# A fifth pair of k tiles in the seven-product scheme of six units of a transformer block kernel

## The chip, the core and the metric

The kernel runs on one core of a Trainium2 chip. The metric is the device time of one launch in microseconds; lower is better. The kernel before took 1368.11 us, the median of three runs (1367.73, 1368.11 and 1368.4).

## The reference, cut to what matters

One block of a hybrid encoder over 256 tokens and 2048 channels, all in float32: a normed input goes through one wide projection, a gated recurrence and a banded attention run side by side, their outputs are merged by gates and projected, and an MLP with a squared ReLU follows. The change lies in the MLP, which is about half of the time:

```python
u = rms_norm(h, norm_mlp_w[l])
h = h + jnp.square(jax.nn.relu(u @ w_up[l])) @ w_down[l]     # (256,2048)@(2048,8192), (256,8192)@(8192,2048)
return rms_norm(h, norm_final_w)
```

## The kernel before

**Three matmuls for one product.** Each float32 factor is split into a rounded part (`wh`, or `hi` on the token side) and the rest (`wl`, `lo`), and `mm3` (L139 to L142) adds hi·wh, hi·wl and lo·wh: L140, L141 and L142, always in that order. One matmul is 128x128 by 128x512.

**Splitting the weights.** A raw block of weights, 128x1024 float32 or 512 KB (two k tiles by 512 columns), comes by one DMA that SyncE (SP) issues (`piece`, L216). ScalarE (ACT) casts it to `wh` (L91), VectorE (DVE) subtracts to get `wl` (L92); `parts` (L221) does this, in buffers that `buf` (L202) hands out. `wh` and `wl` have four buffers each; after the gates' units begin, every fifth block gets a buffer in a further pool, `fifths`, so that there are five. The cast of a block can't start before TensorE (PE) has read the last of the block whose buffer it takes.

**A unit** (`class Unit`, L782, and `run`, L895) makes a 256x1024 output over 16 k tiles: 2 by 2 output banks c11, c12, c21, c22. The first 8 k tiles go through a seven-product scheme of Strassen's kind: with the k tiles as two halves of four, each product is four k tiles times 512 columns, and the unit needs 7 of them, 7 x 4 x 3 = 84 matmuls, where 8 would be the plain way. They are named by bank and weight block, in this order: 11A, 22A, then 12C and 11D (either first), 21A, 21B, 21D. The weight blocks A, B, C, D are two raw tiles each, numbered 0 and 2. DVE adds A += B and A += C in place (`sums`, L851, L854); GpSimd (POOL) sends B += C and D += A as adding DMAs (`sent`, L856). On the token side the combinations are the tiles S5, S4, S2 and S7 made by `combos` (L743). k tiles 8 to 15 go the plain way, two at a time for both token halves: 8 items (`ITEMS`, L780) of 12 matmuls, shown as r1_8, r0_12 and so on (column half, first k tile). That is 84 + 96 = 180 matmuls for a unit.

**Order.** It is written out in `run`, and Tile's scheduler moves what `high_priority` and `issue_after` let it. The last two items of a unit (k tiles 12, 13 and 14, 15 of the second column half) are kept in the list `late` and run inside the next unit, behind its products 11A and 22A; they cover the ACT copies of c11 into c21 and c22 into c12 (`begun`, L831, through L812). When all outputs of a unit are there, ACT evicts them: a ReLU and a square for the up projection (L1208, L1209), a copy `y` for the down projection (L1219), which POOL adds to memory.

**The units of the MLP** follow one another as up00, up02, dn00, dn02, up10, up12, dn10, dn12, up20, up22, dn20, dn22, up30, up32, dn30, dn32: four quarters of the 8192 hidden channels, each with two units up and two down. In the second up and the first down unit of a quarter PE also turns the hidden activations (`turns`, L1189; L110), and ACT and DVE split them. `finals` (L1263) loads the last norm's weights in dn30.

Of the kernel before, what the change touches and what calls it, by code (L numbers as in the profile page):

```python
# [50 lines left out]
def tile_hybrid_block(  # L51
# [691 lines left out]
    def combos(lhs, what, home, made, blocks=None):  # L743

        a = {}

        def block(m, j):
            if blocks:
                a[m, j] = blocks[m, j]
                return  # L750
            a[m, j] = fours(token(f"a{m}{j}_{what}"))
            x = lhs[j][:, :, :, m * P:(m + 1) * P].bitcast(F32)
            nc.vector.tensor_tensor(a[m, j], x[:, :, 0, :], x[:, :, 1, :], op=ALU.add)

# [26 lines left out]

    class Unit:  # L782


        def __init__(self, lhs, S, w, n0, what, done, kt0=0, apart=NC, steps=lambda: (), start=5, fresh=None, held=False, tail=False):
# [4 lines left out]
            self.raw, self.dma, self.c, self.items, self.steps = {}, {}, {}, list(ITEMS), []  # L790

        def load(self, name):
# [3 lines left out]
                              for g in (0, 2)]  # L796

# [97 lines left out]
    def run(u, then=None):  # L895
# [18 lines left out]
        if not late and not u.spread:  # L914
# [24 lines left out]
        u.plain(1, (8, 9))  # L939
# [10 lines left out]
        u.plain(1, (10, 11))  # L950
# [6 lines left out]
        if then:  # L957
            then.load("B")
            then.load("C")
        u.step(next(at))  # L960
        u.plain(0, (8, 9))
# [4 lines left out]
        u.plain(0, (10, 11))  # L966
# [5 lines left out]
        if then:  # L972
            then.load("D")
        if u.tail:
# [22 lines left out]
        late.append(lambda: u.plain(1, LATE[0]))  # L997
# [4 lines left out]
    for f in combos(xT, "x", tk, Sx):  # L1002
# [82 lines left out]

    homes["fifth"] = ctx.enter_context(tc.tile_pool(name="fifths", bufs=1, reuse_waits="tile"))
# [52 lines left out]
    def h_blocks(n0):  # L1139

        def one(n, m):
# [7 lines left out]
            with tc.high_priority(offset=2000):  # L1149
                nc.vector.tensor_tensor(tmp, tp, bc(wmlp[:, 4 * n:4 * n + 4], 2, P), op=ALU.mult)  # L1150
                split(hi[:, :, m * P:(m + 1) * P], lo[:, :, m * P:(m + 1) * P], tmp)
# [33 lines left out]
    for qd in range(NQ):  # L1185
# [3 lines left out]
        def turns(c0, uT=uT, rs=rs, Su=Su, blocks=blocks, qd=qd):  # L1189

            def one(c, m):
# [7 lines left out]
                split(hi[:, :, m * P:(m + 1) * P], lo[:, :, m * P:(m + 1) * P], tp)  # L1199

            return [(c, lambda c=c, m=m: one(c, m)) for c in (c0, c0 + 1) for m in range(NM)] + [
                (c0 + 1, f, 7) for f in ([] if c0 else combos(uT, f"u{qd}", tk, Su, blocks))]

        for c in range(0, 4, 2):
            def done(m, n, acc, c=c, rs=rs, qd=qd):
                t = token(f"r{qd}{c}{n}{m}")
                with tc.high_priority(offset=2000):
# [5 lines left out]
                              steps=(lambda turns=turns: turns(0)) if c else (lambda: ()) if qd else (lambda: h_blocks(2)), start=3 if c else 0, held=not qd and not c))  # L1213
# [49 lines left out]
        def finals():  # L1263
# [3 lines left out]
            nc.scalar.activation(fin["w"], fin["w"], AF.Copy, scale=D ** 0.5)  # L1267
# [4 lines left out]

        for n0 in (0, 2):
            units.append(Unit(lambda uT=uT: uT, lambda Su=Su: Su, w_down, n0 * NC, f"dn{qd}{n0}",
                              lambda m, n, acc, *c, n0=n0, out_of=out_of: out_of(m, n0 + n, acc, *c), kt0=qd * KD,
                              steps=(lambda: ()) if n0 else (lambda turns=turns, last=last: turns(2) + [(3, finals)] * last),
                              start=0, tail=last and n0 == 2))

    for u, then in zip(units, units[1:] + [None]):
# [45 lines left out]
```

## Time and profile before

| | us |
|---|---|
| median of three runs | 1368.11 |
| the profiled execution | 1367.7 |
| its span, first to last instruction | 1366.0 |
| PE busy | 1356.6 (99%) |
| DVE busy | 1122.2 (82%) |
| ACT busy | 948.5 (69%) |
| one unit without transposes (up10) | 40.80 |

The profiled execution is 1.7 us longer than its span and 0.4 us below the median. A matmul is listed with 0.39 us, but it overlaps its neighbours: the next one starts 0.23 us later, and it is this step that counts. For DVE and ACT the same holds in a smaller way: in a row of back-to-back operations the steps are a little shorter than the durations.

### The profile page before, as it was taken

The page shows a single profiled execution, that of the slowest core. Times are in us where ns is not written, and L with a number is a line of the kernel's source. Part 1 is how long each engine was busy: PE and PEld are TensorE (multiplying, and loading weights), DVE is VectorE, ACT ScalarE, POOL GpSimd, SP SyncE. Part 2 cuts the span into 40 slices and gives each one's busy share as a digit, 9 for nine tenths or more (in the row PEclk, how much of TensorE's full clock was granted, in tenths as well). Part 3 has the DMA queues.
Part 4 walks back from the last instruction along what each step waited for, and adds up shares of the span by engine and source line. Part 5 has one row for each costly group of instructions (what it writes and reads, how often), then busy time and mean ns, then how long its engine had stood idle before and what let it go on. Part 6 is the DMA issues. An engine that isn't in the chain of part 4 may idle for free.

```text
span 1366.0 us, 19039 instructions
## 1 busy us (share of the span) xinstructions
PE 1356.6 (99%) x6787; PEld 1123.0 (82%) x6787; DVE 1122.2 (82%) x1302; ACT 948.5 (69%) x1247; POOL 150.1 (11%) x231
## 2 busy tenths in 40 slices
PE   9999999999999999999999999999999999999997
PEld 8888888878778888888888888888888888888886
DVE  7888977887788775798998987789787888878885
ACT  6877765776777664456678766687666876668864
POOL 4000000111111000010121111100111002110210
PEclk9999999999999999999999999999999999999999
DMA  9655557788886996569899889998899888998892
GB/s 333 240 186 156 181 177 264 216 221 244 260 225 169 293 296 210 182 154 324 284 265 269 235 260 295 283 256 244 250 278 298 250 253 237 286 296 258 269 281 98
DMA packets 128895, 333.75 MB, mean 244 GB/s; under 512 B 11152, under 2 KB 12176, under 8 KB 128416
## 3 DMA queue, kind: packets, MB, share of 16 engines
q1 hardware_dynamic: 108080, 265.85, 56.2%
q0 software_dynamic: 20144, 66.14, 24.7%
q8 instruction: 53, 0.87, 0.2%
q10 hardware_dynamic: 576, 0.55, 0.1%
q14 instruction: 42, 0.34, 0.1%
HBM read 271.67 MB, written 10.49 MB: 207 GB/s over the span
## 4 chain that ended last, share of the span: by engine, by line
PE 99%; DMA 1%; ACT 0%; POOLq 0%; issue 0%; POOL 0%
PE acc_hq L182 2%; PE acc_hf L182 2%; PE tp_u L110 1%; PE acc_hg L142 1%; PE acc_hi L142 1%; PE acc_hg L140 1%; PE acc_bb L140 1%; PE acc_hi L141 1%; PE acc_hf L187 1%; PE acc_ba L142 1%; PE acc_hg L141 1%; PE acc_bb L142 1%; PE acc_ba L140 1%; PE acc_ba L141 1%; PE acc_hi L140 1%; PE acc_bb L141 1%
## 5 line engine op out<-in xcount | busy, mean ns | idle before, releaser
L182 PE MATMUL acc_hf<-act_x,wh_hf 128*128 128x512 f32 x128 | 40.9, 401 | 0.6 <-ACT wh_hf L91 0.6
L182 PE MATMUL acc_hq<-act_x,wh_hq 128*128 128x512 f32 x128 | 40.8, 399 | 0.2 <-ACT wh_hq L91 0.2
L91 ACT CAST wh_bb<-raw_bb 128x1024 fp32r<-128x1024 f32 x16 | 16.9, 1054 | 23.3 <-PE acc_ba L142 17.7
L92 DVE TENSOR_TENSOR wl_bb<-raw_bb,wh_bb 128x1024 fp32r<-128x1024 f32 x16 | 19.6, 1223 | 14.8 <-ACT wh_bb L91 14.8
L91 ACT CAST wh_ba<-raw_ba 128x1024 fp32r<-128x1024 f32 x16 | 16.9, 1053 | 19.9 <-PE acc_bb L142 13.8
L92 DVE TENSOR_TENSOR wl_ba<-raw_ba,wh_ba 128x1024 fp32r<-128x1024 f32 x16 | 19.6, 1223 | 10.8 <-ACT wh_ba L91 10.8
L187 PEld LDWEIGHTS acc_hf<-act_x,wl_hf 128*128 128x128 f32 x128 | 23.4, 189 | 5.7 <-DVE wl_hf L92 0.5
L187 PEld LDWEIGHTS acc_hq<-act_x,wl_hq 128*128 128x128 f32 x128 | 23.4, 188 | 5.2
L1220 POOL DMA_DIRECT2D hd<-y x24 | 26.2, 1171 | 1.8 <-ACT y L1219 1.3
L92 DVE TENSOR_TENSOR act_u<-tp_u,act_u 128x512 fp32r<-128x512 f32 x32 | 21.9, 684 | 4.7 <-ACT act_u L91 4.2
L140 PE MATMUL acc_bb<-wh_bb,act_yb 128*128 128x512 f32 x64 | 25.2, 393 | 0.0
L140 PE MATMUL acc_hg<-wh_hg,act_x 128*128 128x512 f32 x64 | 25.1, 392 | 0.0
L140 PE MATMUL acc_hi<-wh_hi,act_x 128*128 128x512 f32 x64 | 25.0, 391 | 0.0
L142 PE MATMUL acc_hg<-wh_hg,act_x 128*128 128x512 f32 x64 | 24.9, 390 | 0.0
L142 PE MATMUL acc_ba<-wh_ba,act_ya 128*128 128x512 f32 x64 | 24.9, 389 | 0.0
L142 PE MATMUL acc_hi<-wh_hi,act_x 128*128 128x512 f32 x64 | 24.9, 389 | 0.0
L141 PE MATMUL acc_hi<-wl_hi,act_x 128*128 128x512 f32 x64 | 24.9, 389 | 0.0
L141 PE MATMUL acc_hg<-wl_hg,act_x 128*128 128x512 f32 x64 | 24.9, 389 | 0.0
L140 PE MATMUL acc_ba<-wh_ba,act_ya 128*128 128x512 f32 x64 | 24.9, 389 | 0.0
L141 PE MATMUL acc_ba<-wl_ba,act_ya 128*128 128x512 f32 x64 | 24.9, 389 | 0.0
L141 PE MATMUL acc_bb<-wl_bb,act_yb 128*128 128x512 f32 x64 | 24.9, 389 | 0.0
L142 PE MATMUL acc_bb<-wh_bb,act_yb 128*128 128x512 f32 x64 | 24.9, 389 | 0.0
(1996 smaller groups left out, 5220.2 us busy)
## 6 DMA issues: line engine op xcount, KB each, us to landing
raw_hi<-in_w_in_n_dram SPq DMA_DIRECT2D x16, 512.0 KB, 4.2
raw_hg<-in_w_in_n_dram SPq DMA_DIRECT2D x16, 512.0 KB, 3.6
raw_ba<-in_w_branch_a_dram SPq DMA_DIRECT2D x16, 512.0 KB, 4.5
raw_bb<-in_w_branch_b_dram SPq DMA_DIRECT2D x16, 512.0 KB, 4.5
raw_hf<-in_w_in_t_dram SPq DMA_DIRECT2D x12, 512.0 KB, 4.1
raw_hq<-in_w_in_t_dram SPq DMA_DIRECT2D x12, 512.0 KB, 5.3
hd<-y POOLq DMA_DIRECT2D x24, 256.0 KB, 7.5
raw_aq<-in_w_in_t_dram SPq DMA_DIRECT2D x8, 512.0 KB, 4.5
```

What stands on the lines that cost most here:

```text
L91: casts[:] = [(copy or nc.scalar.copy)(hi, src)]
L92: low[:] = [nc.vector.tensor_tensor(lo, src, hi.bitcast(F32), op=ALU.subtract)]
L110: nc.tensor.transpose(tp[:, j, :], src[:, j * P:(j + 1) * P], ident)
L140: nc.tensor.matmul(acc, hi, wh, start=first, stop=False, skip_group_check=True)
L141: nc.tensor.matmul(acc, hi, wl, start=False, stop=False, skip_group_check=True)
L142: newest[:] = [nc.tensor.matmul(acc, lo, wh, start=False, stop=last, skip_group_check=True)]
L182: newest[:] = [nc.tensor.matmul(acc[cb], wh[:, cb * P:(cb + 1) * P], r.rearrange("p u t -> p (u t)"), start=kt == 0, stop=last)]
L187: newest[:] = [nc.tensor.matmul(acc[cb][:, 0:T], wl[:, cb * P:(cb + 1) * P], r[:, 0, :], start=False, stop=False)]
L1220: nc.gpsimd.dma_start(hd[n][m], t, accum_op=ALU.add)
```

## The change

Six units (up10, up20, up30, dn02, dn12 and dn22) take a fifth pair of k tiles into the seven products: k tiles 8 and 9. Each product then has five k tiles, 15 matmuls, and only 6 plain items stay (`ITEMS5`): 7 x 15 + 6 x 12 = 177 matmuls.

- The weights of k tiles 8 and 9 come as two raw blocks of 512 KB: X (k tile 8: A5 and B5) and Y (k tile 9: D5 and C5), each 512 columns of a block. They lie in the `fifths` pool, in the place of the fifth `wh` and the fifth `wl` buffer (`load5`). So from unit dn00 to unit up30, eleven units, the split buffers are four and not five (`homes["extra"]`).
- Each product has a third, half-wide split of 128x512 (`half`), which takes a whole buffer.
- The sums of the fifth blocks are DVE additions of 128x512 (`add5`): A5 += B5, A5 += C5, D5 += A5, B5 += C5.
- On the token side `fifths` makes the fifth combinations, one tile S9, once for h (in dn02) and once a quarter for the hidden activations (in dn00, dn10, dn20). Its place is that of S7, which moves into a part of the split activations that no product reads (token half 1 of the first four k tiles). That part is therefore not split any more for h and the hidden activations, and for x S7 is made after the product that still reads it.
- A five-pair unit leaves one late item for the next unit and not two; the next unit then runs 11D ahead of 12C. The addition A += C is placed behind the first of these two products.
- `finals` no longer scales the last norm's weights; a step behind it does (`rooted`).

```diff
-    homes = {}
+    homes = {"extra": False}
...
-        if "fifth" in homes:
-            taken[tag] += 1
-        last = taken[tag] > 0 and taken[tag] % 5 == 0
+        taken[tag] += homes["extra"]
+        last = homes["extra"] and taken[tag] % 5 == 0
...
+    def half(raw, what):
+
+        made = [buf(t, what)[:, 0:NC] for t in ("wh", "wl")]
+        with tc.high_priority(offset=2000):
+            lows.append(split(*[t.rearrange("p (c n) -> p c n", n=T) for t in made], raw))
+        return made
...
-            t = home.tile([P, 4, 2, P], F32R, name=f"S{i}_{what}", tag=f"S{i}", bufs=1)
+            if i == 7:
+                t = lhs[0][:, :, :, P:2 * P]
+            else:
+                t = home.tile([P, 4, 2, P], F32R, name=f"S{i}_{what}", tag=f"S{i}", bufs=1)
...
+    def fifths(lhs, what, home, made):
+
+        a = token(f"a9_{what}").rearrange("p (j t) -> p j t", t=T)
+        x = lhs[2][:, 0:2].bitcast(F32)
+        nc.vector.tensor_tensor(a, x[:, :, 0, :], x[:, :, 1, :], op=ALU.add)
+        c = fours(token(f"c9_{what}"))
...
+        t = home.tile([P, 4, 2, P], F32R, name=f"S9_{what}", tag="S7", bufs=1)
+        split(t[:, :, 0, :], t[:, :, 1, :], c)
+        for k, i in enumerate((5, 7, 2, 4)):
+            made[i].append([t[:, k, u, :] for u in range(2)])
...
+    ITEMS5 = [(1, (10, 11)), (1, (12, 13)), (0, (10, 11)), (0, (12, 13)), (0, (14, 15)), (1, (14, 15))]
+    SUMS5 = {("22", "A"): ("A", "B"), ("21", "A"): ("A", "C"), ("21", "B"): ("B", "C")}
...
+        def load5(self, name):
+            if not self.five:
+                return
+            raw = homes["fifth"].tile([P, 2 * NC], F32, name=f"raw5{name}_{self.what}", tag=("wh", "wl")[name == "Y"], bufs=1)
+            ncols = self.w.shape[-1]
+            k, kpr = self.kt0 + 8 + (name == "Y"), 4 * NC // ncols
+            nc.sync.dma_start(raw.rearrange("p (c n) -> p c n", n=ncols),
+                              self.w[self.n0 // ncols:(self.n0 + 2 * NC) // ncols, k // kpr, :, k % kpr, :].rearrange("c p n -> p c n"))
+            for i, block in enumerate({"X": "AB", "Y": "DC"}[name]):
+                self.raw[f"{block}5"] = raw[:, i * NC:(i + 1) * NC].rearrange("p (c n) -> p c n", n=T)
+
+        def add5(self, dst, src):
+            dst, src = [self.raw[f"{name}5"] for name in (dst, src)]
+            with tc.issue_after(lows[-1].ins), tc.high_priority(offset=2000):
+                nc.vector.tensor_tensor(dst, dst, src, op=ALU.add)
...
+                if not g and self.five and (i, name) in SUMS5:
+                    self.add5(*SUMS5[i, name])
                 for a in range(2):
                     mm3(self.c[i], *left(g + a), wh[:, a], wl[:, a], first and not g + a, False)
+            if self.five:
+                mm3(self.c[i], *left(4), *half(self.raw[f"{name}5"], f"{self.what}p{i}{name}5"), False, False)
+                if (i, name) == ("21", "A"):
+                    self.add5("D", "A")
...
-        if not late and not u.spread:
+        if len(late) < 2 and not u.spread:
             seconds.reverse()
...
         seconds[0]()
+        behind_first = lows[-1]
         u.step(next(at))
         seconds[1]()
         with ExitStack() as es:
-            if u.spread:
-                es.enter_context(tc.issue_after(lows[-1].ins))
+            if u.spread or u.five:
+                es.enter_context(tc.issue_after((behind_first if u.five else lows[-1]).ins))
             u.sums("A", "C")
...
             then.load("B")
             then.load("C")
+            then.load5("X")
...
         if then:
             then.load("D")
+            then.load5("Y")
...
-        late.append(lambda: u.plain(1, LATE[0]))
+        if not u.five:
+            late.append(lambda: u.plain(1, LATE[0]))
         late.append(rest)
...
-                split(hi[:, :, m * P:(m + 1) * P], lo[:, :, m * P:(m + 1) * P], tp)
+                if c or not m:
+                    split(hi[:, :, m * P:(m + 1) * P], lo[:, :, m * P:(m + 1) * P], tp)
...
+        def rooted():
+            with tc.issue_after(casts[0].ins):
+                nc.scalar.activation(fin["w"], fin["w"], AF.Copy, scale=D ** 0.5)
...
-    for u, then in zip(units, units[1:] + [None]):
+    lent = [i for i, u in enumerate(units) if u.five]
+    for i, (u, then) in enumerate(zip(units, units[1:] + [None])):
+        homes["extra"] = not lent[0] - 1 <= i <= lent[-1]
         run(u, then)
```

How the instructions stand, at two places of unit up10. First DVE, from the splits of the third product on; `wl_up10p12C0` is the split of the weight tile C0 for product 12C, `wl_up10r1_8` that of a plain item, `raw_up10A2<-raw_up10A2,raw_up10C2` an addition A += C. Before:

```order
L92 TENSOR_TENSOR wl_up10p22A2_8042<-raw_up10A2_7831,wh_up10p22A2_8041 128x1024
L92 TENSOR_TENSOR wl_dn02r1_14_8054<-rawp_dn02r1_14_7899,wh_dn02r1_14_8053 128x1024
L854 TENSOR_TENSOR raw_up10A2_7831<-raw_up10A2_7831,raw_up10C2_7880 128x1024
L92 TENSOR_TENSOR wl_up10p12C0_8078<-raw_up10C0_7878,wh_up10p12C0_8077 128x1024
L92 TENSOR_TENSOR wl_up10p12C2_8088<-raw_up10C2_7880,wh_up10p12C2_8087 128x1024
L92 TENSOR_TENSOR wl_up10p11D0_8098<-rawd_up10D0_7937,wh_up10p11D0_8097 128x1024
L92 TENSOR_TENSOR wl_up10p11D2_8108<-rawd_up10D2_7939,wh_up10p11D2_8107 128x1024
L92 TENSOR_TENSOR wl_up10r1_8_8122<-rawp_up10r1_8_7973,wh_up10r1_8_8121 128x1024
L92 TENSOR_TENSOR wl_up10p21A0_8140<-raw_up10A0_7829,wh_up10p21A0_8139 128x1024
```

And in the changed kernel, from the split of 22A's fifth tile (A5, in the X block) to that of 21A0:

```order
L92 TENSOR_TENSOR wl_up10p22A5_8119<-raw5X_up10_7942,wh_up10p22A5_8118 128x512
L92 TENSOR_TENSOR wl_up10p11D0_8130<-rawd_up10D0_7988,wh_up10p11D0_8129 128x1024
L92 TENSOR_TENSOR wl_up10p11D2_8140<-rawd_up10D2_7990,wh_up10p11D2_8139 128x1024
L92 TENSOR_TENSOR wl_up10p11D5_8150<-raw5Y_up10_7992,wh_up10p11D5_8149 128x512
L905 TENSOR_TENSOR raw_up10A0_7883<-raw_up10A0_7883,raw_up10C0_7938 128x1024
L92 TENSOR_TENSOR wl_up10p12C0_8157<-raw_up10C0_7938,wh_up10p12C0_8156 128x1024
L92 TENSOR_TENSOR wl_up10p12C2_8167<-raw_up10C2_7940,wh_up10p12C2_8166 128x1024
L92 TENSOR_TENSOR wl_up10p12C5_8177<-raw5Y_up10_7992,wh_up10p12C5_8176 128x512
L905 TENSOR_TENSOR raw_up10A2_7885<-raw_up10A2_7885,raw_up10C2_7940 128x1024
L92 TENSOR_TENSOR wl_up10r1_10_8188<-rawp_up10r1_10_8026,wh_up10r1_10_8187 128x1024
L92 TENSOR_TENSOR wl_up10p21A0_8206<-raw_up10A0_7883,wh_up10p21A0_8205 128x1024
```

The late item r1_14 has left this place, 11D stands ahead of 12C, two half-wide splits have come in, and both additions A += C now stand in front of the first plain item's split, one of them right in front of it.

Second PE, at the same first plain item of up10. Before, from the last matmuls of 11D:

```order
L140 MATMUL acc_up10c11_7985<-wh_up10p11D2_8107,act_h1_6333 128x512
L141 MATMUL acc_up10c11_7985<-wl_up10p11D2_8108,act_h1_6333 128x512
L142 MATMUL acc_up10c11_7985<-wh_up10p11D2_8107,act_h1_6333 128x512
L140 MATMUL acc_up10c12_8051<-wh_up10r1_8_8121,act_h2_6618 128x512
L141 MATMUL acc_up10c12_8051<-wl_up10r1_8_8122,act_h2_6618 128x512
L142 MATMUL acc_up10c12_8051<-wh_up10r1_8_8121,act_h2_6618 128x512
```

And in the changed kernel, from the fifth tile of 12C (with S9 on the token side):

```order
L140 MATMUL acc_up10c12_8125<-wh_up10p12C5_8176,S9_h_7849 128x512
L141 MATMUL acc_up10c12_8125<-wl_up10p12C5_8177,S9_h_7849 128x512
L142 MATMUL acc_up10c12_8125<-wh_up10p12C5_8176,S9_h_7849 128x512
L140 MATMUL acc_up10c12_8125<-wh_up10r1_10_8187,act_h2_6613 128x512
L140 MATMUL acc_up10c22_8096<-wh_up10r1_10_8187,act_h2_6613 128x512
L140 MATMUL acc_up10c21_8066<-wh_up10p21A0_8205,S2_h_6444 128x512
L141 MATMUL acc_up10c12_8125<-wl_up10r1_10_8188,act_h2_6613 128x512
L142 MATMUL acc_up10c12_8125<-wh_up10r1_10_8187,act_h2_6613 128x512
```

Two matmuls that need only `wh` have been moved ahead of the first that needs r1_10's `wl`: it is now the fourth of the item's row and not the second.

## Rows read from the trace of the kernel before

**Rows 1.** The page: busy time of PE, and its granted clock in 40 slices.
```profile
PE 1356.6 (99%) x6787; PEld 1123.0 (82%) x6787; DVE 1122.2 (82%) x1302; ACT 948.5 (69%) x1247; POOL 150.1 (11%) x231
PEclk9999999999999999999999999999999999999999
```

**Rows 2.** The page: the chain that ended last, by engine.
```profile
PE 99%; DMA 1%; ACT 0%; POOLq 0%; issue 0%; POOL 0%
```

**Rows 3.** Waits of PE, whole span: us in total, times, longest.
```profile
PE ps_warm L81 <- DVE warm L79: 1.1, 1, 1.1
PE acc_hf L182 <- ACT wh_hf L91: 0.6, 1, 0.6
PE acc_hq L182 <- ACT wh_hq L91: 0.2, 1, 0.2
```

**Rows 4.** Windows of up10, up12, dn10, ga0: busy us (instructions), PEclk, DMA share, GB/s.
```profile
851.38:892.18 40.80, 40.80 (x181) 33.78 (x180) 31.21 (x28) 27.39 (x31) 6.82 (x8) 1.00 0.98 279
892.18:935.01 42.83, 42.83 (x197) 35.31 (x196) 38.95 (x41) 34.44 (x46) 3.40 (x4) 1.00 0.85 249
935.01:977.73 42.72, 42.72 (x197) 35.35 (x196) 35.49 (x34) 31.32 (x39) 3.85 (x5) 1.00 0.88 249
336.11:383.92 47.81, 47.81 (x241) 38.48 (x240) 38.41 (x44) 35.91 (x56) 5.81 (x11) 1.00 0.84 235
```

**Rows 5.** Timeline of PE in up10: start us, us, engine, line, operation.
```profile
862.26 0.39 PE L140 MATMUL acc_up10c<-wh_up10p12C,S_h 128*128 128x512 f32 x1
862.49 0.39 PE L141 MATMUL acc_up10c<-wl_up10p12C,S_h 128*128 128x512 f32 x1
...
864.98 0.39 PE L140 MATMUL acc_up10c<-wh_up10p11D,act_h 128*128 128x512 f32 x1
...
867.93 0.39 PE L141 MATMUL acc_up10c<-wl_up10r,act_h 128*128 128x512 f32 x1
```

**Rows 6.** Timeline of ACT in up10; in brackets idle us before, and what ended it.
```profile
862.46 0.59 ACT L1219 COPY y<-acc_dn02c 128x512 f32<-128x512 f32 x1 [0.64 <-PE acc_dn02c L142]
862.95 1.05 ACT L91 CAST wh_up10r<-rawp_up10r 128x1024 fp32r<-128x1024 f32 x1
...
865.18 1.06 ACT L91 CAST wh_up10p21A<-raw_up10A 128x1024 fp32r<-128x1024 f32 x1 [0.24 <-PE acc_up10c L142]
```

**Rows 7.** Timeline of DVE in up10.
```profile
854.29 1.22 DVE L92 TENSOR_TENSOR wl_dn02r<-rawp_dn02r,wh_dn02r 128x1024 fp32r<-128x1024 f32 x1
855.43 1.22 DVE L854 TENSOR_TENSOR raw_up10A<-raw_up10A,raw_up10C 128x1024 f32<-128x1024 f32 x1
856.57 1.22 DVE L92 TENSOR_TENSOR wl_up10p12C<-raw_up10C,wh_up10p12C 128x1024 fp32r<-128x1024 f32 x1
...
864.03 1.23 DVE L92 TENSOR_TENSOR wl_up10r<-rawp_up10r,wh_up10r 128x1024 fp32r<-128x1024 f32 x1 [1.44 <-ACT wh_up10r L91]
```

**Rows 8.** Timeline of DVE in up12: operations of 512 columns.
```profile
917.38 0.68 DVE L92 TENSOR_TENSOR act_u<-tp_u,act_u 128x512 fp32r<-128x512 f32 x1
917.98 0.69 DVE L842 TENSOR_TENSOR acc_up12c<-acc_up12c,u_up 128x512 f32<-128x512 f32 x1
918.57 1.21 DVE L92 TENSOR_TENSOR wl_up12r<-rawp_up12r,wh_up12r 128x1024 fp32r<-128x1024 f32 x1
```

**Rows 9.** Timeline of unit ga0, which has four buffers: a split, and its reader.
```profile
337.97 1.23 DVE L92 TENSOR_TENSOR wl_ga0p22A<-raw_ga0A,wh_ga0p22A 128x1024 fp32r<-128x1024 f32 x1 [0.56 <-ACT wh_ga0p22A L91]
...
340.42 0.39 PE L141 MATMUL acc_ga0c<-wl_ga0p22A,S_x 128*128 128x512 f32 x1
```

**Rows 10.** Timeline of PE in up12: the transposes.
```profile
908.51 1.03 PE L110 MATMUL tp_u<-ident,r 128*128 128x128 f32 x8
909.30 0.48 PE L140 MATMUL acc_up12c<-wh_up12r,act_h 128*128 128x512 f32 x1
909.61 0.40 PE L141 MATMUL acc_up12c<-wl_up12r,act_h 128*128 128x512 f32 x1
```

**Rows 11.** Loads: one DMA group of the page's kind, and raw_up10A's time to landing.
```profile
rawp_up10r<-in_w_up_dram SPq DMA_DIRECT2D x8, 512.0 KB, 6.5
...
DMA to landing us min/median/max: 5.6/6.9/11.3
```

**Rows 12.** Timeline of ACT in dn30: the last norm's weights.
```profile
1292.74 1.91 ACT L1267 ACTIVATE wf<-wf 128x2048 f32<-128x2048 f32 x1
```

More of the change, by code (lines that the diff above doesn't have):

```diff
@@ L780, in tile_hybrid_block, with __init__ @@
     ITEMS = [(1, (8, 9)), (1, (10, 11)), (0, (8, 9)), (0, (10, 11)), (0, (12, 13)), (0, (14, 15))] + [(1, ks) for ks in LATE]
+    ITEMS5 = [(1, (10, 11)), (1, (12, 13)), (0, (10, 11)), (0, (12, 13)), (0, (14, 15)), (1, (14, 15))]
+    SUMS5 = {("22", "A"): ("A", "B"), ("21", "A"): ("A", "C"), ("21", "B"): ("B", "C")}
     class Unit:
-        def __init__(self, lhs, S, w, n0, what, done, kt0=0, apart=NC, steps=lambda: (), start=5, fresh=None, held=False, tail=False):
+        def __init__(self, lhs, S, w, n0, what, done, kt0=0, apart=NC, steps=lambda: (), start=5, fresh=None, held=False, tail=False, five=False):
             self.lhs, self.S, self.w, self.n0, self.what, self.done = lhs, S, w, n0, what, done
@@ L789, in __init__ @@
             self.spread, self.fresh = fresh is not None, fresh or ()
-            self.raw, self.dma, self.c, self.items, self.steps = {}, {}, {}, list(ITEMS), []
+            self.raw, self.dma, self.c, self.items, self.steps = {}, {}, {}, list(ITEMS5 if five else ITEMS), []
+            self.five = five
         def load(self, name):
@@ L938, in run @@
         u.step(next(at))
-        u.plain(1, (8, 9))
+        u.plain(1, (10, 11) if u.five else (8, 9))
         item(u)
@@ L949, in run @@
         u.step(next(at))
-        u.plain(1, (10, 11))
+        u.plain(1, (12, 13) if u.five else (10, 11))
         u.less("12", u1)
@@ L959, in run @@
             then.load("C")
+            then.load5("X")
         u.step(next(at))
-        u.plain(0, (8, 9))
+        u.plain(0, (10, 11) if u.five else (8, 9))
         u.less("22", u2)
@@ L965, in run @@
         u.step(next(at))
-        u.plain(0, (10, 11))
+        if not u.five:
+            u.plain(0, (10, 11))
         u.residual("11")
@@ L995, in rest @@
             u.end(1)
-        late.append(lambda: u.plain(1, LATE[0]))
+        if not u.five:
+            late.append(lambda: u.plain(1, LATE[0]))
         late.append(rest)
     Sx = {}
-    for f in combos(xT, "x", tk, Sx):
+    x_sums = combos(xT, "x", tk, Sx)
+    for f in x_sums[:3]:
         f()
@@ L1054, in tile_hybrid_block @@
         scaled("k0", rstd, m, acc_k[m])
+    x_sums[3]()
     yb += [new_act(f"yb{g}") for g in range(2)]
@@ L1150, in one @@
                 nc.vector.tensor_tensor(tmp, tp, bc(wmlp[:, 4 * n:4 * n + 4], 2, P), op=ALU.mult)
-                split(hi[:, :, m * P:(m + 1) * P], lo[:, :, m * P:(m + 1) * P], tmp)
+                if n or not m:
+                    split(hi[:, :, m * P:(m + 1) * P], lo[:, :, m * P:(m + 1) * P], tmp)
             nc.scalar.activation(tp.rearrange("p k t -> p (k t)"), t, AF.Square, accum_out=ssq2[:, m, n:n + 1])
@@ L1198, in one @@
                     nc.scalar.copy(blocks[m, c], tp)
-                split(hi[:, :, m * P:(m + 1) * P], lo[:, :, m * P:(m + 1) * P], tp)
+                if c or not m:
+                    split(hi[:, :, m * P:(m + 1) * P], lo[:, :, m * P:(m + 1) * P], tp)
             return [(c, lambda c=c, m=m: one(c, m)) for c in (c0, c0 + 1) for m in range(NM)] + [
-                (c0 + 1, f, 7) for f in ([] if c0 else combos(uT, f"u{qd}", tk, Su, blocks))]
+                (c0 + 1, f, 7) for f in ([] if c0 else combos(uT, f"u{qd}", tk, Su, blocks))] + [
+                (99, lambda: fifths(uT, f"u{qd}", tk, Su), 7)] * (c0 > 0 and qd < NQ - 1)
         for c in range(0, 4, 2):
@@ L1212, in tile_hybrid_block @@
             units.append(Unit(lambda: hT, lambda: Sh, w_up, qd * (FF // NQ) + c * NC, f"up{qd}{c}", done,
-                              steps=(lambda turns=turns: turns(0)) if c else (lambda: ()) if qd else (lambda: h_blocks(2)), start=3 if c else 0, held=not qd and not c))
+                              steps=(lambda turns=turns: turns(0)) if c else (lambda: ()) if qd else (lambda: h_blocks(2)), start=3 if c else 0, held=not qd and not c, five=qd > 0 and not c))
         def out_of(m, n, acc, c=slice(0, NC), last=last, qd=qd):
@@ L1275, in tile_hybrid_block @@
                               lambda m, n, acc, *c, n0=n0, out_of=out_of: out_of(m, n0 + n, acc, *c), kt0=qd * KD,
-                              steps=(lambda: ()) if n0 else (lambda turns=turns, last=last: turns(2) + [(3, finals)] * last),
-                              start=0, tail=last and n0 == 2))
-    for u, then in zip(units, units[1:] + [None]):
+                              steps=(lambda qd=qd: [(99, lambda: fifths(hT, "h", sp, Sh))] * (not qd)) if n0 else (lambda turns=turns, last=last: turns(2) + [(3, finals), (99, rooted, 9)] * last),
+                              start=3 if n0 else 0, tail=last and n0 == 2, five=n0 == 2 and not last))
+    lent = [i for i, u in enumerate(units) if u.five]
+    for i, (u, then) in enumerate(zip(units, units[1:] + [None])):
+        homes["extra"] = not lent[0] - 1 <= i <= lent[-1]
         run(u, then)
```

9 lines of the change are left out of this document (7 added, 2 removed).

## The prediction

> **What bounds the kernel now.** I began with the page: PE is busy for 1356.6 of 1366.0 us, and its granted clock is at the upper level, 2.4 GHz, in all 40 slices [rows 1]. The chain that ended last is 99% PE [rows 2]. PE's waits, asked for next, are three, 1.9 us in all, none in the MLP [rows 3]. So the time of the MLP is its matmuls by the step from one to the next. The windows give the step; their columns are the length, the busy time of PE, PEld, DVE, ACT and POOL, and the clock, DMA share and GB/s. Unit up10 takes 40.80 us for 180 matmuls: 0.2267 us each [rows 4]. Where PE never waits, a product left out is worth its matmuls, as long as nothing new is late. So I read in timelines how far ahead of PE the splits are.
>
> **How near the splits are.** In up10 the split of the first plain item starts at 864.03, takes 1.23 and ends at 865.26 [rows 7]; PE's first matmul that reads it is at 867.93 [rows 5]. The lead is 2.67 us. Its path: PE leaves the buffer at 862.26 (the next piece's first matmul) [rows 5]; an eviction copy starts at 862.46, 0.20 later, and holds ACT until the cast starts at 862.95; the split starts 1.08 after that [rows 6, 7]. So release to split is 1.28 us without a copy in the way and 1.77 with one; 1.28 agrees with the other cast in the rows, which starts 0.20 after its matmul (864.98, 865.18) [rows 5, 6]. Operations in a row on DVE step by 1.14 us at 1024 columns (854.29, 855.43, 856.57) and by 0.60 at 512 (917.38, 917.98, 918.57) [rows 7, 8]; listed durations are 1.22 and 0.68.
>
> **The change, part by part.**
>
> *Matmuls.* Six units go from 180 to 177: 18 x 0.2267 = -4.08 us. This is the whole gain; a unit should take 40.12.
>
> *DVE in these units.* 22 splits of 1024 become 20, seven of 512 and four additions of 512 come in: -2 x 1.22 + 11 x 0.68 = +5.0 us. With up10's 31.21 [rows 4] that is about 36 of 40.1. ACT gets seven casts of 512 for two of 1024, at most 7 x 0.59 - 2 x 1.05 = +2.0 on 27.39 [rows 4, 6], with 0.59 the duration of a copy. Neither is full on the mean; the question is one tight place.
>
> *The tight place of the up units (up10, up20, up30).* Count from the first matmul of 11A. PE's row, in matmuls: 11A 15, late item r1_14 12, 22A 15, 11D 15, 12C 15, then the item r1_10. With four buffers 11D0 takes that of r1_14, which PE leaves after 27 matmuls, at 6.12 us. With a copy in the way the split of 11D0 starts at 6.12 + 1.77 = 7.89. By the order shown, DVE then has six operations of 1024 (11D0, 11D2, A0 += C0, 12C0, 12C2, A2 += C2) and two of 512 (11D5, 12C5) before r1_10: 7.89 + 6 x 1.14 + 2 x 0.60 = 15.93, and r1_10's split ends at 17.15. PE wants it as the fourth matmul of the item, after 75: 17.00. So it is 0.15 late. On the way 12C0 ends at 7.89 + 3 x 1.14 + 0.60 + 1.22 = 13.13 against 58 matmuls, 13.15: no room either. By the listed durations instead of the steps the row lasts 8.68 and r1_10 ends at 17.79, 0.79 late; were no copy in the way, 0.34 early. So 0 to 0.8 a unit; I take 0.25, nearer to the steps, since back to back is what the rows show. Three units: +0.75. In the kernel before the cover here was the second late item, 12 matmuls or 2.72 us; it is gone.
>
> *The down units (dn02, dn12, dn22)* still get two late items, and 12C goes first. The same sum with 12 more matmuls ahead leaves 11D0, here behind 12C and both additions, some 0.5 early. 0 to 0.3, taken 0.03 each: +0.1.
>
> *Five plain units with four buffers (dn00, up12, dn10, up22, dn20).* Pessimistically, a buffer less costs the lead of one plain item, 12 matmuls: 2.67 - 2.72 = -0.05. But ga0, on four buffers already, is the nearest row: a split there ends at 337.97 + 1.23 = 339.20, its reader is at 340.42, a lead of 1.22 [rows 9], and PE waits nowhere in it [rows 3]. I take 0; 0 to 0.3 each.
>
> *Transposes.* In up12, up22, up32 and up02 fewer items or another order puts the groups as 8 transposes, 8 matmuls, 8 and 4 instead of 8, 10, 4, 1, 4, 1. A group's change costs a little: eight transposes start at 908.51, the next matmul is at 909.30 and the one behind it 0.31 later, not 0.23 [rows 10]. up12 is 42.83 long against up10's 40.80, 2.03 us for 16 transposes [rows 4]; two groups of 0.79 would be 1.58 and a third change 0.1 to 0.2. I take -0.2 in up02 and up32, which have five buffers: -0.4; all four within -1.0 and +0.3.
>
> *Token side.* The fifth combinations are an addition and a split of 512, a cast, and four narrow additions, 2 to 2.5 us of DVE, in dn00, dn10, dn20 and dn02; one split of 0.68 is dropped for h and each quarter. dn10 has 42.72 - 35.49 = 7.2 us of DVE free [rows 4], and nothing reads S9 before the next five-pair unit. 0, bounds 0 and 0.3 each. S7 of x, moved behind another product: 0 for the same reason.
>
> *The norm's weights.* Their scaling, 1.91 us of ACT in dn30 [rows 12], now stands ahead of an activation copy that PE's transposes and combinations hang on. Up to its length less what leads there are: 0 to 0.3, taken 0.1.
>
> *Loads.* Bytes stay. X and Y are issued on SP's queue behind C and D. X's place is free when 21B's half-wide split is done, and X is wanted at least 66 matmuls, 15.0 us, later; blocks of this size land in 6.5 us, at worst 11.3 [rows 11]. Hidden; SP's later loads stand one or two issues further back, with the same lead.
>
> *Sum.* -4.08 + 0.75 + 0.1 - 0.4 + 0.1 = -3.5 us, of which I keep -3.4, for the token side. From the profiled execution's 1367.7 that gives 1364.3; it lies 0.4 below the median, so 1364.7 on the scale of 1368.11.
>
> **The rivals.**
>
> *A: the gain is eaten.* All tight places at their upper ends: three up units x 0.8, three down x 0.3, five plain units x 0.1, the norm 0.3, no gain at the transposes: -4.08 + 2.4 + 0.9 + 0.5 + 0.3 = 0.0; with some of it, 1367.5. For it: 12C0 and r1_10 have no lead by my count. Against it: it needs listed durations where rows show shorter steps.
>
> *B: four buffers are too few (slower).* In a product with a half-wide split the three buffers behind the released one hold 6 + 6 + 3 matmuls, 3.40 us. A new split needs 1.77 + 1.22 = 2.99 from the release [rows 5 to 7]. The margin is 0.41 us; a second copy on ACT (0.49) or one DVE operation ahead (0.60) ends it, and PE then stalls again and again. At 0.3 us in three places in eleven units: +9.9 - 4.1 gives about 1374. It decides from some 14 such stalls on. The whole stretch has the lent buffers, not only the six units. Against it: ga0's wait-free run [rows 3, 9], though it has no half-wide splits, and plain units hold 18 matmuls, 4.08 us, behind a release. The Trainium skill, "Perfetto Trace Analysis", Optimization Strategy, speaks for this rival: the same gap repeating on the engine that should be saturated can mean that there is too little memory for the next tile. No run here shows such gaps yet.
>
> *C: X comes too late (slower).* X is fetched in runs of 1 KiB in the up units where the blocks before had 2 KiB, and the DMA share in up10 is already 0.98 [rows 4]. If a block took twice the worst landing, 22.6 us, PE would stand for 7.6 in each up unit: 1364.7 + 22.8 = 1387; it decides from 15.0 us to landing on. At twice the median, 13.0, nothing is seen. Against it: X is one block in 16, and its lead is over twice the median. The same page's section DMA Optimizations says that transfers under 2 KB carry a significant overhead each; by it X would be slower to land, but it gives no time that could be set against 15.0.
>
> *The change doing nothing* is out: the three matmuls a unit are gone from PE's row.
>
> **How the numbers follow.** Forecast 0.62, A 0.26, B 0.09, C 0.03. What can be told from no change is 0.2%, 2.7 us: faster is below 1365.4, slower above 1370.8. The forecast's own range is 1363.2 (no stall, -0.8 at the transposes) to 1366.0; its upper part, about 0.04, is within 0.2%, and about as much of A and B's lighter sides lies to either side. Faster 0.61, same 0.28, slower 0.11. The range goes on through A to 1368.6 and leaves out B, C and 0.05 below or between.
>
> **What would show it.** Right: from 11A to the next 11A the six units take 40.1 to 40.9 us; PE's new waits are for DVE, on 12C0 or r1_10 in up10, up20 and up30, 0.1 to 0.8 each, and hardly any elsewhere; DVE's busy time in up10 is 35 to 36; up12 and dn10 stay within 0.3 of before. Wrong: waits of PE for a cast in many units (B), ACT waiting for the X or Y block's DMA (C), a granted clock below 1.00 behind a stall, or six units at 40.1 with no wait at all, which would mean that DVE's row is shorter than I counted.

## The result: slower by 0.23%

The changed kernel takes 1371.76 us, the median of 16 runs, against 1368.22 us of the kernel before, 16 runs beside them: a ratio of 1.0023, 95% interval 1.0017 to 1.0030. That is 3.5 us slower where 3.4 us faster were forecast, and 3.2 us above the forecast's range.

The page of the profiled execution still shows PE busy all the time [rows 1], but the chain that ended last is no longer PE alone [rows 2]:

```profile
PE 1356.5 (99%) x6769; PEld 1120.3 (82%) x6769; DVE 1149.2 (84%) x1375; ACT 958.9 (70%) x1276; POOL 150.0 (11%) x231
...
PE 94%; DMA 2%; DVE 1%; ACT 1%; issue 1%; POOL 0%; POOLq 0%; DVEq 0%; ACTq 0%
```

18 matmuls are gone (6769 for 6787), and PE's busy time is the same to 0.1 us: a PE that steps slowly is busy too. The waits of PE name two places that were not there before [rows 3], both in up30 (us in total, times, longest):

```profile
PE acc_up30c L140 <- ACT wh_up30r L91: 1.5, 1, 1.5
PE acc_hf L182 <- ACT wh_hf L91: 1.3, 1, 1.3
PE ps_warm L81 <- DVE warm L79: 1.1, 1, 1.1
PE acc_up30c L141 <- DVE wl_up30r L92: 0.9, 1, 0.9
```

The windows from 11A to the next unit's 11A say how much (up10, up12, dn12, up30; columns as in [rows 4]). A unit's stretch takes in the late items of the unit before: dn12 has two, up10 and up30 one, so up10 and up30 hold 177 matmuls, 40.13 us at 0.2267 each, and dn12 189, 42.85 us. up12 takes in one and leaves two: 168 matmuls, and its 16 transposes.

```profile
854.84:895.28 40.44, 40.44 (x179) 33.07 (x178) 35.79 (x38) 29.87 (x36) 6.92 (x9) 1.00 1.04 294
895.28:935.41 40.13, 40.13 (x186) 33.09 (x184) 37.07 (x39) 33.34 (x45) 3.44 (x5) 1.00 0.90 271
978.13:1020.98 42.85, 42.85 (x191) 35.49 (x190) 36.99 (x39) 30.03 (x36) 6.57 (x9) 1.00 0.93 251
1187.11:1231.99 44.88, 42.40 (x178) 34.02 (x177) 37.60 (x39) 30.08 (x36) 7.55 (x10) 0.96 0.95 268
```

By these counts dn12 has no stall at all, up10 (and up20) 0.3 us, and up30 4.75 us. From dn02's 11A to dn30's the units take 460.06 us against 458.69 before. With 18 matmuls less that stretch should be 4.08 shorter; it is 1.37 longer, so 5.45 us were lost, 4.75 of them in up30. Outside it the profiled execution has 1.4 us more ahead of dn02, 0.1 in dn30 and 0.9 from dn32's start to the end.

What happened in up30 stands in ACT's timeline:

```profile
1216.93 0.62 ACT L91 CAST wh_up30p21D<-raw5Y_up 128x512 fp32r<-128x512 f32 x1
1221.74 2.94 ACT L91 CAST wh_up30r<-rawp_up30r 128x1024 fp32r<-128x1024 f32 x3 [4.19 <-DMA rawp_up30r<-in_w_up_dram]
1224.59 1.99 ACT L91 CAST wh_up32p11A<-raw_up32A 128x1024 fp32r<-128x1024 f32 x2
```

ACT stands for 4.19 us until a load lands, and then makes three casts in a row: the last two items were there, and could not pass. The program's order says which cast stood in front. ACT's row in the changed kernel:

```
L91 CAST wh_up30p21D5_11254<-raw5Y_up30_10914 128x512
L91 CAST wh_up30r1_14_11332<-rawp_up30r1_14_11125 128x1024
L91 CAST wh_up30r0_12_11265<-rawp_up30r0_12_11016 128x1024
L91 CAST wh_up30r0_14_11281<-rawp_up30r0_14_11049 128x1024
```

The first of the three plain items, r1_14, is the late item: it is the unit's last load on SP's queue, and PE needs it last of the three, inside up32. Its cast got the fifth `wh` buffer, which is given back for up32. That is the place of the X block, free as soon as 21B's half-wide split has read X; so, unlike the other two, this cast had no matmul to wait for, and it was put ahead of them. PE then ran dry (timeline of PE):

```profile
1221.88 0.39 PE L142 MATMUL acc_up30c<-wh_up30p21D,act_h 128*128 128x512 f32 x1
1223.79 0.50 PE L140 MATMUL acc_up30c<-wh_up30r,act_h 128*128 128x512 f32 x1 [1.53 <-ACT wh_up30r L91]
1225.24 0.79 PE L141 MATMUL acc_up30c<-wl_up30r,act_h 128*128 128x512 f32 x1 [0.95 <-DVE wl_up30r L92]
1225.83 0.63 PE L142 MATMUL acc_up30c<-wh_up30r,act_h 128*128 128x512 f32 x1
1226.26 0.63 PE L140 MATMUL acc_up30c<-wh_up30r,act_h 128*128 128x512 f32 x1
```

and came back at the lower clock (windows of 1 us; 0.50 is the level of 1.2 GHz):

```profile
1226.00:1227.00 1.00, 1.00 (x4) 0.81 (x3) 1.00 (x2) 0.58 (x1) 0.00 (x0) 0.50 0.88 324
...
1228.00:1229.00 1.00, 1.00 (x5) 0.84 (x4) 1.00 (x2) 0.00 (x0) 0.00 (x0) 0.89 0.96 205
```

The three starts after 1221.88 come 1.91, 1.45 and 0.59 us apart instead of 0.23, 3.3 us beyond the usual; then steps of 0.43 cost another 1.2 us until the clock is back. Sum 4.5, the difference between up30 and up10.

### The profile page after: what moved, and what is told of

Read it like the earlier page. It is cut to its first block, busy times and chain, and to the rows that moved or that the text cites. A ratio compares the mean times of both kernels' runs of the same rounds, so it can differ in the third digit from the quotient of the medians.

```text
span 1369.8 us, 19126 instructions
## 1 busy us (share of the span) xinstructions
PE 1356.5 (99%) x6769; PEld 1120.3 (82%) x6769; DVE 1149.2 (84%) x1375; ACT 958.9 (70%) x1276; POOL 150.0 (11%) x231
## 4 chain that ended last, share of the span: by engine, by line
PE 94%; DMA 2%; DVE 1%; ACT 1%; issue 1%; POOL 0%; POOLq 0%; DVEq 0%; ACTq 0%
PE acc_hq L182 2%; PE acc_hf L182 2%; PE tp_u L110 1%; PE acc_hf L187 1%; PE acc_hg L140 1%; PE acc_hi L140 1%; PE acc_bb L140 1%; PE acc_hi L142 1%; PE acc_hg L142 1%; PE acc_ba L142 1%; PE acc_bb L142 1%; PE acc_ba L140 1%; PE acc_hg L141 1%; PE acc_ba L141 1%; PE acc_bb L141 1%; PE acc_ga2c L140 1%
## 5 line engine op out<-in xcount | busy, mean ns | idle before, releaser
L182 PE MATMUL acc_hq<-act_x,wh_hq 128*128 128x512 f32 x128 | 40.9, 399 | 0.2 <-ACT wh_hq L91 0.2
L187 PE MATMUL acc_hf<-act_x,wl_hf 128*128 128x256 f32 x128 | 24.7, 279 | 0.0
```

Of the source, the lines that this page charges most:

```text
L182: newest[:] = [nc.tensor.matmul(acc[cb], wh[:, cb * P:(cb + 1) * P], r.rearrange("p u t -> p (u t)"), start=kt == 0, stop=last)]
L187: newest[:] = [nc.tensor.matmul(acc[cb][:, 0:T], wl[:, cb * P:(cb + 1) * P], r[:, 0, :], start=False, stop=False)]
```

## The experiments

Theory: a cast out of turn in up30 holds ACT, and that is the whole swing. Rivals: the loads themselves are pushed back by X and Y; four split buffers are too few. The times are medians; the kernel before had 1368.6 us beside the first four, 1368.6 beside the next four and 1369.9 beside the last.

### e1_lent_longer and e2_cast_in_turn: the late item back in its place, two ways

```diff
-        homes["extra"] = not lent[0] - 1 <= i <= lent[-1]
+        homes["extra"] = not lent[0] - 1 <= i <= lent[-1] + 1      # e1
```
```diff
+        held = casts[0].ins                                        # e2
         def rest():
-            u.plain(1, LATE[1])
+            with ExitStack() as es:
+                if u.what == "up30":
+                    es.enter_context(tc.issue_after(held))
+                u.plain(1, LATE[1])
```

> The changed kernel, but the split buffers stay four for one unit more, through up32, so that the late item of up30 gets an ordinary buffer. Theory: the loss sits in up30, where this late item got the fifth buffer, free early; its cast was put ahead of those of r0_12 and r0_14 and ACT, which works in order, stood 4.2 us for its load. Then up30 takes 40.4 us instead of 44.9, no PE wait there, and the kernel some 1367.3 (kernel before 1368.2, changed 1371.8). Rival: the DMA is full (share 0.9 and more) and X and Y push the plain items' loads back; then ACT waits in up30 for another load just as long and the time stays at 1371 to 1372. Second rival, four buffers are too few: a unit more of them makes it worse, 1372 or more.

> The changed kernel; the cast of up30's late item r1_14 may only be issued behind that of r0_14, buffers as in the changed kernel. ACT's row differs in this place and one copy behind it, DVE's in the matching split, nothing in the loads. Theory: up30 40.4 us, no PE wait in it, clock 1.00 throughout, the kernel 1367.3 and its runs closer together than the changed kernel's. Rival (loads pushed back by X and Y): still 1371 or more, since the loads are the same.

e1 took 1367.10 us (ratio to before 0.9989, 0.9981 to 0.9998), e2 1367.18 (0.9994, 0.9985 to 1.0002). In e2 not one load changed its place. On ACT and DVE this cast and its split did, with a few operations of up32 behind them, and on PE one matmul of up32. up30 is as long as up10:

```profile
1187.00:1227.44 40.44, 40.44 (x179) 33.07 (x177) 35.46 (x38) 29.95 (x37) 5.88 (x7) 1.00 1.02 295
```

ACT there takes the items in the order of their loads, held only for its split buffers until the last (timeline of ACT in e2):

```profile
1218.57 1.05 ACT L91 CAST wh_up30r<-rawp_up30r 128x1024 fp32r<-128x1024 f32 x1 [1.35 <-PE acc_up30c L142]
1219.93 1.06 ACT L91 CAST wh_up30r<-rawp_up30r 128x1024 fp32r<-128x1024 f32 x1 [0.30 <-PE acc_up30c L142]
1221.62 1.05 ACT L91 CAST wh_up30r<-rawp_up30r 128x1024 fp32r<-128x1024 f32 x1 [0.63 <-DMA rawp_up30r<-in_w_up_dram]
```

The cast of the late item, the last of these, starts when its load lands, 34.9 us after up30's first matmul; in the changed kernel that was 34.6. So the load did not come sooner; it no longer stood in front. 4.0 (e2) to 4.7 us (e1) of the changed kernel's 1371.8 by the ratios, 4.6 by the medians, hang on the place of one cast. What is left is small: e1 is 0.02 to 0.19% faster than the kernel before, and e2 can't be told from it. That the runs would lie closer together did not come true: e2's go from 1365.4 to 1370.8.

### e3_before_four and e5_before_four_turn: four split buffers alone

```diff
-        if "fifth" in homes:
-            taken[tag] += 1
-        last = taken[tag] > 0 and taken[tag] % 5 == 0
+        taken[tag] += homes["extra"]
+        last = homes["extra"] and taken[tag] % 5 == 0
...
+        homes["extra"] = not 4 <= i <= 14          # units dn00 to up30 (e3, of the kernel before)
```

> The kernel before, without any fifth pair, but with four split buffers from dn00 to up30 as in the changed kernel. PE's row is the same. Theory: four buffers cost nothing to 0.1 us a unit, 1368.2 to 1369.3; in up30 the cast of the late r1_12 moves one place ahead of r0_14's, which may cost ACT about 1 us of waiting and PE nothing. Rival (four buffers too few): PE waits for DVE or ACT in most of the eleven units, 1370 or more.

1376.02 us (ratio 1.0057, 1.0042 to 1.0071): the theory was wrong here. Four buffers in the old layout cost up10 0.9, up12 0.4, up20 0.5, up22 0.5 and up30 3.45 us in the profiled execution (1373.68, the shortest of the six), and the six down units 0 to 0.14 each. In up30 both causes meet, for here too the first late item's cast had moved ahead of r0_14's:

```profile
ACT wh_up30r L91 <- DMA rawp_up30r<-in_w_up_dram: 9.6, 3, 4.0
PE acc_up30c L140 <- ACT wh_up30r L91: 1.4, 1, 1.4
PE acc_up30c L141 <- DVE wl_up30r L92: 0.9, 1, 0.9
```

e5 holds that cast behind r0_14's, as e2 does:

> As e3_before_four (kernel before, four split buffers from dn00 to up30, 1376.0), but in up30 the cast of the late r1_12 comes behind r0_14's, in the order of their loads. Theory of casts out of turn: the 3.45 us that up30 took beyond 40.8 in e3 fall to the 0.5 to 0.9 that up10 and up20 took, so some 2.5 us go and the kernel is at 1373 to 1374. Rival: up30's excess comes from late loads as in up10 and up20 and only grew there; then it stays near 3 and the kernel at 1375 to 1377.

1373.89 us (ratio 1.0040, 1.0027 to 1.0052); up30 44.25 to 41.67, 2.6 us, as expected. (up32 became 1.2 us longer, with a wait of the transposes for a split of the activations; the hold shifts a few operations there too.) So a cast out of turn costs PE time in another kernel too, and the rest, 0.4 to 0.9 in each up unit, is something else.

### e6_down_only: why does the changed kernel not pay for its four buffers?

```diff
-                              ... held=not qd and not c, five=qd > 0 and not c))
+                              ... held=not qd and not c, five=False))          # up units plain again; dn22's late cast held
```

> The changed kernel with the fifth pair in dn02, dn12 and dn22 alone (9 matmuls fewer than before), four buffers from dn00 to dn22, casts of dn22's late item held in turn. Question: why do four buffers cost the old layout 6 us in e3 and the changed one next to nothing. Theory of the loads: with four buffers a split comes later, so its raw buffer comes free later and the next plain load lands later; in the changed kernel's up units X and Y, fetched a unit ahead, take two plain loads out of this row. Then here, where the up units have eight plain loads again, up10 and up20 get waits of ACT for plain loads and PE stalls of 0.4 to 1 us and the units behind them 0.4; -2.0 + 2.5 and the 1 us at start and end that e1 and e2 show: 1368.5 to 1370. Rival: the changed kernel's late-item order and not the loads keeps the up units whole; then no stall in up10 and up20, 1366.5 to 1367.5.

1382.39 us (ratio 1.0096, 1.0081 to 1.0112): the direction of the theory of the loads, at several times its price. up10 took 45.20 us for 168 matmuls (38.09), up20 43.78 and up30 39.86. Waits in up10, and the time to landing of its plain loads, which was 4.5/6.5/9.1 in the kernel before:

```profile
ACT wh_up10r L91 <- DMA rawp_up10r<-in_w_up_dram: 7.0, 1, 7.0
PE acc_up10c L140 <- ACT u_up L857: 4.3, 1, 4.3
```
```profile
DMA to landing us min/median/max: 5.2/8.9/13.2
```

ACT stands for a plain load (r0_10), and the copy that PE needs is queued behind it. The plain casts stand in the order of their loads here; this load went out 15.2 us after up10's first matmul, where the kernel before had 13.9, and was slower to land. The rival is out, for up10 has the changed kernel's late-item order here and stalls. So X and Y in the up units do not cause such a stall; the changed kernel, which has them, has none. That it has none because X and Y are fetched a unit ahead, and six plain loads stand in the tight row instead of eight, is inferred; no run isolates it.

### e9_before_four_lend: only the loads moved

e5, with the two empty places as a fourth and fifth raw buffer for plain loads:

```diff
+        if tag == "rawp" and homes.get("lend"):                    # dn00 to dn20
+            taken[tag] = taken.get(tag, 0) + 1
+            if taken[tag] % 5 > 2:
+                pool, bufs, place = homes["fifth"], 1, ("wh", "wl")[taken[tag] % 5 - 3]
```

> As e5_before_four_turn (kernel before with four split buffers from dn00 to up30, 1373.9), but the two places that stand empty there serve as a fourth and a fifth raw buffer for the plain items' loads of dn00 to dn20 and dn22's first. The rows of PE, DVE, ACT and POOL stay word for word; only SP issues these loads sooner. Theory of the loads: what four buffers cost there is the load that is issued later; then up10 goes from 41.70 to 40.8 to 41.0, up12 from 43.11 to 42.9, up20 and up22 likewise (41.44, 43.30), 2 to 2.5 us in all, and up30 (41.67) and up32 (43.99), whose loads are not eased, keep theirs: 1371.4 to 1372. Rival: the splits themselves come too late for PE with four buffers, whatever the loads do; then up10, up12, up20 and up22 stay as in e5 and the kernel at 1373.9. Second rival: the DMA has no more to give, earlier loads only delay others, and the time grows.

1372.68 us (ratio 1.0021, 1.0011 to 1.0031). SP issued up10's first plain load 6.5 us ahead of up10's first matmul in the kernel before, 3.1 in e5 and 12.8 in e9 (timelines of SP, in this order):

```profile
844.92 10.98 SPq L216 DMA_DIRECT2D rawp_up10r<-in_w_up_dram  x3
848.58 10.84 SPq L215 DMA_DIRECT2D rawp_up10r<-in_w_up_dram  x3
841.72 0.63 SPq L220 DMA_DIRECT2D rawp_up10r<-in_w_up_dram  x1
```

The windows of up10 in e5, then of up10 in e9, and of up30 in e9, whose loads were not eased:

```profile
851.65:893.35 41.70, 41.22 (x182) 33.63 (x180) 31.50 (x29) 27.08 (x31) 6.75 (x8) 1.00 0.98 275
854.47:895.26 40.79, 40.79 (x181) 33.78 (x180) 32.16 (x29) 27.50 (x31) 6.94 (x9) 1.00 1.01 291
1189.70:1231.76 42.06, 41.39 (x182) 33.62 (x180) 31.73 (x29) 26.66 (x30) 6.93 (x8) 1.00 0.97 272
```

up10, up12, up20 and up22 are back at 40.80, 42.81, 40.80 and 42.83, within 0.02 of what five buffers gave (40.80 and 42.83 in [rows 4], 40.80 and 42.81 for up20 and up22), with the rows of the four engines the same as in e5. So what a missing split buffer costs there is the load: a split made later frees its raw buffer later, and the load issued into it lands too late. (The four units won 2.3 us; the kernel won 1.2 by the medians and 2.6 by the ratios. In its profile dn22, just behind the lent stretch, took 0.9 longer and up30 0.4.) The Trainium skill, "Perfetto Trace Analysis", Optimization Strategy, says that the same gap repeating can mean too little memory for the next tile; in e5 it did (41.70 against e9's 40.79 in up10), but the tile that was short is the raw one of the load, one step ahead of the one that PE waited for.

### e4_a2_later and e8_sums_behind: the additions moved

Of e2, A2 += C2 behind r1_10's split in the up units (e4), or both additions behind the second product's last split (e8):

```diff
-            u.sums("A", "C")
+            u.sums("A", "C", slice(0, 1) if one else slice(0, 2))
...
+        if one:
+            with tc.issue_after(lows[-1].ins):
+                u.sums("A", "C", slice(1, 2))                       # e4
```
```diff
-                es.enter_context(tc.issue_after((behind_first if u.five else lows[-1]).ins))
+                es.enter_context(tc.issue_after(lows[-1].ins))      # e8
```

> As e2_cast_in_turn; besides, in up10, up20 and up30 the second addition A2 += C2 (and the adding DMA behind it) comes after the split of the first plain item r1_10 and not before it. Theory of the row on DVE: r1_10's split starts 1.14 us sooner, PE's wait for it goes (some 0.1 to 0.15 us a unit), the one for 12C0 stays; a unit takes 40.2 to 40.35 instead of 40.43, the kernel 0.3 to 0.5 below e2. Rival: D += A comes later by 3 us and 21D's cast waits for it; then up units get longer.

> As e2_cast_in_turn (1367.2), but the two additions A += C come behind the second product's last split on DVE and not behind the first's. Theory of the row on DVE: 12C0's and 12C2's splits in up10, up20 and up30 are done 1.14 us sooner and the PE stall of some 0.3 a unit falls to that at r1_10, 0.1 or less; up units 40.2, the kernel 0.5 lower at best. Rival from e4: whatever delays A2 and the adding DMA D += A lengthens the landings of the next unit's loads (13 to 17 us instead of 9 to 11 in e4); then up12, up22 and up32 get longer by 0.5 to 2 us and the kernel is at 1368.5 or more.

e4: 1370.14 us (1.0007, 0.9999 to 1.0016). up10 is 40.32 instead of 40.44, the small gain as expected, and up12 41.37 instead of 40.12, up22 40.94 instead of 40.31, up32 42.48 instead of 40.14. SP's row changed with the buffers, and up12's plain loads took up to 17.2 us to land; in e2 the same line reads 5.2/7.1/11.5:

```profile
DMA to landing us min/median/max: 4.0/8.0/17.2
```

That the late landings cause up12's loss is inferred; no run isolates it. e8: 1374.51 us (1.0041, 1.0027 to 1.0055). up12, up22 and up32 were longer (41.46, 40.81 and 42.60), as its rival said. What neither theory nor rival had: the two additions came in front of r1_10's split, 1.14 us each, and every five-pair unit, up and down, got a new stall there, 0.5 us in up10 (PE):

```profile
875.50 0.39 PE L140 MATMUL acc_up10c<-wh_up10p21A,S_h 128*128 128x512 f32 x1
876.44 0.50 PE L141 MATMUL acc_up10c<-wl_up10r,act_h 128*128 128x512 f32 x1 [0.55 <-DVE wl_up10r L92]
```

The place that the change gives A += C is the better one of the two.

### e7_four_to_end: never back to five

```diff
-        homes["extra"] = not lent[0] - 1 <= i <= lent[-1]
+        homes["extra"] = i < lent[0] - 1
```

> The changed kernel with four buffers from dn00 to the end, so that no late item meets a fifth buffer. Theory of casts out of turn: up30 40.4 us as in e1. With eight plain loads in up32 and four buffers the theory of the loads expects about 0.4 us more there and up to 1 in dn30 and dn32: 1367 to 1368.5. Rival (four buffers are too few by themselves): the last three units lose 1 us or more each, 1369 or more.

1368.07 us (0.9996, 0.9987 to 1.0005), within the theory's range. up30 40.43 and up32 40.12, without the 0.4 that was expected; from dn32's start to the end it takes 56.1 us, 1.4 more than in e2, where up to 1 was expected.

## Why the prediction was wrong

**The step that failed** is the third up unit of the tight place: "Three units: +0.75", each with 0.25. up10 and up20 had 0.31 and 0.30; up30 had 4.75. The working took up30 for a copy of up10. It is not: its late item runs in a unit with five buffers again. The forecast asked for each operation when PE would release its buffer and when DVE would reach it, and took for granted that ACT makes its casts in the order of their loads. Where the fifth buffer comes back, a cast without a buffer to wait for was put ahead, and in an engine that works in order its load became everybody's. e2 shows it: this cast in turn, 1371.8 to 1367.2. The row of ACT at the seam from four buffers to five, shown above, stands in the program itself; the forecast worked out only one up unit. Of the 7.3 us between its sum (-3.5) and the profiled execution (+3.8), 4.5 are up30, 0.3 the transposes, 1.5 lie ahead of up00 and 0.9 from dn32 on.

**What held.** *Matmuls:* 18 fewer, a unit without a stall at its matmuls times 0.2267 (dn12, 189, at 42.85; up12, 168, at 38.09 and 2.04 for its transposes). *The tight row of DVE:* worked out as 12C0's split ending 13.13 us after 11A's first matmul and r1_10's at 17.15. 11D0's split was to start 7.89 us after it and did (862.73 - 854.84). In up10 of the changed kernel 12C0's starts at 866.74 and r1_10's at 870.75; with 1.22 they end 13.12 and 17.13 us after 854.84:

```profile
866.74 2.35 DVE L92 TENSOR_TENSOR wl_up10p12C<-raw_up10C,wh_up10p12C 128x1024 fp32r<-128x1024 f32 x2
...
870.75 1.22 DVE L92 TENSOR_TENSOR wl_up10r<-rawp_up10r,wh_up10r 128x1024 fp32r<-128x1024 f32 x1
```

Both came just in time for PE, and each still cost it about 0.15: up to 0.03 of waiting, and a first matmul that is followed 0.11 later than the others (12C0):

```profile
868.02 0.50 PE L141 MATMUL acc_up10c<-wl_up10p12C,S_h 128*128 128x512 f32 x1
868.35 0.39 PE L142 MATMUL acc_up10c<-wh_up10p12C,S_h 128*128 128x512 f32 x1
868.58 0.39 PE L140 MATMUL acc_up10c<-wh_up10p12C,S_h 128*128 128x512 f32 x1
```

PEld's load for that first matmul is held for the same split and starts together with the matmul; the loads of its neighbours start about a step of 0.23 ahead of theirs:

```profile
868.01 0.19 PEld L141 LDWEIGHTS acc_up10c<-wl_up10p12C,S_h 128*128 128x128 f32 x1 [0.29 <-DVE wl_up10p12C L92]
868.12 0.19 PEld L142 LDWEIGHTS acc_up10c<-wh_up10p12C,S_h 128*128 128x128 f32 x1
868.36 0.19 PEld L140 LDWEIGHTS acc_up10c<-wh_up10p12C,S_h 128*128 128x128 f32 x1
```

*Busy times:* DVE 35.79 in up10 ("about 36"), ACT 29.87, 0.5 above the most that was worked out (29.4). *Down units:* no stall. *The norm's weights:* dn30 0.1 us longer, as taken.

**Two signs that were drawn wrong.** From 11A to the next 11A the down units take in two late items and leave one, so they took 42.85 us where 40.1 to 40.9 was named, without a stall. up12 holds 12 matmuls less than before and took 40.13 us for 42.83, where "within 0.3" was named. Neither speaks for or against the mechanism. The sign of a granted clock below 1.00 behind a stall was drawn right, and came.

**Held by luck.** The 0.25 of up10 and up20 was r1_10 being 0.15 late, and some more; the 0.3 came from two places with next to no lateness and 0.11 behind each. "Five plain units with four buffers: 0" is right in the changed kernel (up12, dn10: no wait), but its reason, ga0's example, is not: in the old layout the same four buffers cost up10, up12, up20 and up22 0.4 to 0.9 each (e3), through the plain loads (e9). The lead of the splits was counted, that of the plain loads was taken as unchanged, though the DMA share of 0.98 in up10 stood in the rows [rows 4]. *Loads:* in the up units X landed in 8.2 to 9.8 us and Y in 9.6 to 11.5, slower than the 6.5 of before and still well within the 15.0 (X):

```profile
DMA to landing us min/median/max: 8.2/9.1/9.8
```

**Rivals.** B, four buffers too few with PE stalling again and again, gave 1374 and would have come nearest, but not by what happened: one stall, not fourteen. A and C did not occur.

**What stays open.** *Transposes:* of the 0.4 us expected, up02 gave 0.1 and up32, at 40.05, next to nothing. Of the 1.4 us ahead of dn02, 1.0 arises in the first 41 us, at the first loads. It varies: in the changed kernel and its variants, alike up to there, up00 begins between 682.1 and 686.0; the kernel before has 682.3. Of the 0.9 from dn32 on, half lies inside dn32 and half behind the last matmul. That end takes 8.2 to 8.5 us in the changed kernel and four of its variants, 7.7 to 7.8 in the kernel before and the other two; no wait in the trace explains it. In e1 the units by themselves gain 2.7 us, from dn02's 11A to dn30's 456.02 against 458.69; its profiled execution gives back 0.7 ahead of dn02 and 1.1 from dn32 on.

## What to carry to other kernels

Where a change lends a buffer and gives it back, read the order of the engine that fills it at both seams: an instruction that finds a free output buffer early is put early, and in an engine that works in order its input's landing time is then everyone's. Count the leads one step further back than the tiles that PE reads: a split that comes later frees a raw buffer later, and here, at a DMA share of 0.98, the load into that buffer was what PE paid for. When one unit of a pattern stands next to another kind of unit, work it out by itself.

## What the runs showed of the hardware

In up30 three late starts, 3.3 us of stall in all, cost 4.5: the granted clock fell to 0.50 (1.2 GHz) and the steps were 0.43 us for about 2.5 us; in e6 a start 4.6 us behind the one before it was followed by eleven such steps. In up10 a split that was ready just when PE wanted it cost 0.11 us beyond the wait: the load for the first matmul started with it and not ahead of it, and the step behind it was 0.34 and not 0.23. With the DMA share of up10 at 0.98 (e4) and 1.04 (e2), the slowest landing of up12's 512 KB loads was 17.2 us in e4 and 11.5 in e2; the two kernels differ there by one addition placed later by an operation, and the order of the loads that moved with it.
